# Three small pieces of softmax and value work moved off GpSimd in a hybrid mLSTM and sliding-window kernel

## The chip, the cores and the metric

The kernel runs on one core of one Trainium2 chip. The metric is the device time of one execution in microseconds (us); a lower one is better. Several executions are timed, and the median counts. One execution is also recorded by the hardware profiler, and its trace is what the views of the profile are drawn from. The engines are named as in the profile: PE (TensorE, matrix products), PEld (its loading of weights), DVE (VectorE), ACT (ScalarE), POOL (GpSimd) and SP (SyncE, which here issues most of the DMAs).

## The reference, cut to what matters

One layer of a streaming encoder is computed for a prompt of 2048 tokens and for a decoding batch of 8 sequences with 16 new tokens each. The input projection feeds two groups of heads: an mLSTM matrix memory (4 heads of 128), and a sliding-window attention (8 query heads, 2 key and value heads of 64, each query head with a learned sink). An output projection, a layer norm, a convolutional feed-forward part and a second layer norm follow. The two places that the change touches are these:

```python
# mLSTM, per chunk: the numerator and its normaliser
num = w_inter * (q @ C) + s @ v
den = w_inter * (q @ n) + sum(s, axis=-1)
h = num / max(abs(den), exp(-mt))

# attention with a sink
mx = max(max(s, axis=-1), sink)
p = exp(s - mx)
p = p / (sum(p, axis=-1) + exp(sink - mx))
o = p @ v
```

The kernel gets `den` from the same matrix product as `num`: it puts a column of ones behind the 128 columns of each head's values. It gets the sink's part of the sum by putting the sink into one more column behind the scores of the prompt's tiles, so that one exponential with a running sum covers both.

## The kernel before, in words

Tokens are handled in 17 tiles of 128: tiles 0 to 15 are the prompt, tile 16 (`NPT`) is the decoding batch. All products use float32 split into a high and a low part, three matmuls for one.

The work falls into stages. The input projection (L705 and L731 for its matmuls) goes through four blocks of tiles; the output projection (L223 to L225, called from `group`) through five; then come the up projection (L1874) and the down projection (L2081). These dense stages supply most of TensorE's work. The small work of the mLSTM and of the attention is cut into steps and woven into the dense stages by the class `Chains`. It keeps a clock of its own units, `t`: each piece of dense work (six matmuls in the input projection) adds 645 to it. Three chains wait to be stepped: `t_sample` (the decoding batch), `m_chain` (mLSTM, tile by tile) and `a_chain` (attention, tile by tile). A chain's step ends with `yield cost, delay` (and a number of PSUM banks that must be free): `cost` is added to the clock, and the chain is stepped again at the first piece of dense work at which the clock has passed the delay. `m_chain` and `a_chain` wait until `t_sample` is done.

So the order of TensorE's instructions is the order in which Python issues them, written out before the kernel runs (`manual_schedule` names PE alone). The other engines' instructions, and SP's DMAs, are put in order by the framework's scheduler, from the dependences and from the order of the program; every engine then works through its list in order. Tiles of one tag share a fixed number of buffers, and the framework puts in the waits that buffers and data need.

The output projection asks for finished tiles: `x_pair` (L893 issues its load) calls `chains.until(t)`, which steps the chains at once, without dense work between, if tile `t` isn't done. Block 3 of the output projection ends with a pair of tiles, and after the second of eight pieces of that pair's inner sum it asks for tiles 14 and 15.

The places of the change:

- `m_load` loads a tile's queries and keys, values and output gate. L1092 takes a tile `v1` of 4 heads by 129 columns from two buffers, L1093 issues the DMA of 128 columns of each head, L1094 lets GpSimd fill the four last columns with ones. `m_tile` reads `v1` at L1212 and L1221, and `t_sample` at L1438; `weighted` (L1424) takes two more tiles of the tag `v1`.
- `swa` handles one prompt tile of attention in two calls of `scores`, each for four of the eight heads. L1298 lets GpSimd copy the sink (four values per partition) behind the scores; L1304 is the score matmul, L1308 moves scores with mask and maximum to SBUF on VectorE, L1311 forms the negative maximum. `exps` (L1316) takes the exponentials with their sum on ScalarE, `divided` (L1319 the reciprocal, L1321 the scaled copies on ScalarE) divides, L1343 transposes on TensorE, L1344 copies the transposes and L1349 multiplies by the values.
- `swa_sample` does the attention of the decoding batch in two halves of four sequences. L1500 and L1501 are the score matmuls, L1502 to L1508 the maximum, L1509 the exponentials, L1510 and L1511 the sum and its reciprocal, L1512 the division by GpSimd for all four sequences in one instruction (128 partitions x 4 x 144), L1513 the step's end, L1518 and L1519 the transposes.

Of the kernel before, what the change touches and what calls it, by code (L numbers as in the profile page):

```python
# [10 lines left out]
AF = mybir.ActivationFunctionType  # L11
# [3 lines left out]
P = 128  # L15
# [5 lines left out]
NPT = SEQ // P  # L21
NT = NPT + 1
TOK = NT * P
MH = 4
# [181 lines left out]
class Prog:  # L206
# [881 lines left out]
    def m_load(self, t, b, ti):  # L1088
        nc = self.nc
        qk = self.work("qk", [P, 8, P], bufs=2)  # L1090
        nc.sync.dma_start(qk, self.zqk[b][:, :, ti * P:(ti + 1) * P].rearrange("f p m -> p f m"))
        v1 = self.work("v1", [P, MH, 129], bufs=2)  # L1092
        nc.sync.dma_start(v1[:, :, :P], self.zv[t].rearrange("p (h e) -> p h e", h=MH))  # L1093
        nc.gpsimd.memset(v1[:, :, P:129], 1.0)  # L1094
        og = self.work("og", [P, MH, P])
        nc.sync.dma_start(og, self.zog[t].rearrange("p (h e) -> p h e", h=MH))
        return qk, v1, og
# [174 lines left out]
    def swa(self, t):  # L1272
        nc = self.nc
        V = nc.vector
        if self.a_first is None:
            self.swa_first(t)
            yield 550, 4000, 2
        qh, ql = self.a_first
        self.a_first = None
        r = t % RING  # L1280
        if t == 0:
            slots, nk = [0], 1
            mask = self.mswa[:, :P]
            sel = slice(0, 1)
        else:
            slots, nk = sorted([(t - 1) % RING, r]), 2
            mask = self.mswa[:, P:] if slots[1] == r else self.mswa[:, :2 * P]
            sel = slice(slots[0], slots[1] + 1, slots[1] - slots[0])
        N = nk * P
        mix = self.work("mixa", [P, 4, P])  # L1290

        def scores(j0):

            sink, nsink = [x.rearrange("p (k j) -> p k j", k=2)[:, :, j0:j0 + 2] for x in (self.sink, self.nsink)]
            sc = self.work("sc", [P, 4, 2 * P + 4], bufs=2)
            mx, sm = [self.work(n, [P, 4], bufs=2) for n in ("amx", "asm")]
            w = lambda x: x.rearrange("p (k j) -> p k j", k=2)
            nc.gpsimd.tensor_copy(sc[:, :, N:N + 1].rearrange("p (k j) o -> p k (j o)", k=2), sink)  # L1298
            ps = [self.bank([P, 2, 2, P], "psc") for _ in range(2)]
            for j in range(2):  # L1300
                for i, (q, k) in enumerate(((qh, self.kh), (qh, self.kl), (ql, self.kh))):
                    for kvh in range(2):
                        rs = slice(64 * kvh, 64 * kvh + 64)
                        nc.tensor.matmul(ps[kvh][:, j, :nk], q[rs, j0 + j], k[rs, sel], start=i == 0, stop=i == 2)  # L1304
            for kvh in range(2):
                for j in range(2):
                    c = 2 * kvh + j
                    V.tensor_tensor_reduce(out=sc[:, c, :N], in0=ps[kvh][:, j, :nk].rearrange("p a b -> p (a b)"), in1=mask, scale=1.0, scalar=-3e38,  # L1308
                                           op0=ALU.add, op1=ALU.max, accum_out=mx[:, c:c + 1])

            V.scalar_tensor_tensor(w(mx), w(mx), -0.125, nsink, op0=ALU.mult, op1=ALU.min)  # L1311
            return sc, mx, sm

        def exps(sc, mx, sm):
            for j in range(4):
                nc.scalar.activation(sc[:, j, :N + 1], sc[:, j, :N + 1], AF.Exp, bias=mx[:, j:j + 1], scale=0.125, accum_out=sm[:, j:j + 1])  # L1316

        def divided(sc, mx, sm):
            V.reciprocal(sm, sm)  # L1319
            for j in range(4):  # L1320
                nc.scalar.activation(sc[:, j, :N], sc[:, j, :N], AF.Copy, scale=sm[:, j:j + 1])  # L1321

        z = [scores(0)]
        yield 900, 3200, 2
        exps(*z[0])
        z.append(scores(2))
        yield 900, 3600
        exps(*z[1])
        divided(*z[0])
        if t + 1 < NPT and self.i_done > self.place(t + 1)[0]:  # L1330
            self.a_load = self.swa_dma(t + 1)
        yield 0, 3000
        divided(*z[1])
        scs = [x[0] for x in z]
        yield 0, 4200, 2 + 2 * (self.a_load is not None)

        po = pts = None
        for kt in range(nk + 1):
            new = self.work("pth", [P, 2, 512], bufs=2) if kt < nk else None
            for kvh in range(2) if kt < nk else ():  # L1340
                pp = self.bank([P, 512], "ppt")
                for j in range(4):
                    nc.tensor.transpose(pp[:, j * P:(j + 1) * P], scs[j // 2][:, 2 * kvh + j % 2, kt * P:(kt + 1) * P], self.ident)  # L1343
                nc.scalar.copy(new[:, kvh], pp)  # L1344
            if kt:
                po = po or self.bank([P, 512], "ppo")
                for kvh in range(2):
                    w = self.kv[slots[kt - 1]][:, P + 64 * kvh:P + 64 * kvh + 64]
                    nc.tensor.matmul(po[64 * kvh:64 * kvh + 64], w, pts[:, kvh], start=kt == 1, stop=kt == nk)  # L1349
            pts = new  # L1350
            if kt == 0 and self.a_load is not None:

                self.swa_first(t + 1)
                self.chains.t += 550
            yield (860 if kt < nk else 0) + (1400 if kt else 0), 0 if kt == nk else 1500 if kt else 3000, 2 * (kt + 1 < nk) + (kt == 0)
        nc.scalar.copy(mix.rearrange("p a b -> p (a b)"), po)
        self.mix_out(t, 4, mix)
# [113 lines left out]
    def swa_sample(self, load, kvc):  # L1471
        nc, a = self.nc, self.a
        V = nc.vector
        t = NPT
# [9 lines left out]
        NK = P + DS  # L1484
        HB = DB // 2
        sk = self.sinkx.to_broadcast([P, HB])
        for half in range(2):
# [4 lines left out]
            sc = self.work("sc", [P, HB, NK], bufs=2, name="scs")  # L1492
            mx, es, sm = [self.work(n, [P, HB], bufs=2) for n in ("amx", "aes", "asm")]
            for b0 in (0, 2):
                ps = self.bank([P, 2, NK], "pscs")
                for i in range(2):
                    b = half * HB + b0 + i
# [11 lines left out]
                nc.scalar.activation(sc[:, b], sc[:, b], AF.Exp, bias=mx[:, b:b + 1], scale=0.125, accum_out=sm[:, b:b + 1])  # L1509
            V.tensor_add(sm, sm, es)  # L1510
            V.reciprocal(sm, sm)  # L1511
            nc.gpsimd.tensor_mul(sc, sc, sm.rearrange("p (b o) -> p b o", o=1).to_broadcast([P, HB, NK]))  # L1512
            yield 2700, 6500  # L1513
            pts = self.work("pth", [P, 2, HB, P], bufs=2, name="pts")
            pp = self.bank([P, HB, P], "ppt")
            pp2 = self.bank([DS, HB, P], "ppt2")
# [679 lines left out]
```

## Time and profile before

| | |
|---|---|
| median of 3 runs | 2306.43 us (2305.89 to 2309.27) |
| profiled execution, its own time | 2306.25 us |
| span of its trace | 2304.5 us |
| instructions | 39741 |
| granted TensorE clock, mean | 0.997 |

The span is what the trace covers, from its first to its last instruction; the execution's own time has some microseconds around it. A row of a view of groups gives line, engine, operation, the output and inputs by their names and shapes, the count, busy us and mean ns of one, and the idle time of the engine ahead of them with what ended it. A row of a timeline gives start and length in us; an idle time ahead of it and what ended it stand in brackets. In names, `scs` is the decoding batch's scores, `sc` the prompt tiles', `amx` the maxima, `asm` the sums, `v` the values with their ones, `ppt` the transposes' PSUM bank, `dps` the dense products' bank.

### The profile page before, as it was taken

What the parts mean: (1) busy time and instruction counts of PE and PEld (TensorE: products, weight loads), DVE (VectorE), ACT (ScalarE), POOL (GpSimd) and SP (SyncE); (2) the same over time, 40 slices, a digit from 0 to 9 for tenths busy, and PEclk for the clock granted to TensorE, in tenths of its full rate; (3) what the DMA queues carried; (4) which work ended last, traced back from release to release, by engine and by line L of the source; (5) the groups of instructions that cost most, each with busy time, mean ns of one, the idle gap of its engine ahead of it and who ended that gap; (6) DMA issues with size and microseconds to landing.
All of it is one profiled execution on the core that took longest, in us unless ns stands there. A gap on an engine that the chain in (4) does not pass through costs nothing.

```text
span 2304.5 us, 39741 instructions
## 1 busy us (share of the span) xinstructions
PE 2278.9 (99%) x14293; PEld 2094.4 (91%) x14293; DVE 1807.4 (78%) x3075; ACT 1272.4 (55%) x2377; POOL 279.4 (12%) x509
## 2 busy tenths in 40 slices
PE   8999999999999999999999999999999999999998
PEld 8999999989877778999999999999999978888876
DVE  8787587787688888998778777678766786895987
ACT  5453476776766656555656555556555544444442
POOL 0001001100011210211112101003111200200200
PEclk9999999999999999999999999999999999999999
DMA  7988999899987757888777888878998786746742
GB/s 267 319 306 297 309 322 342 310 306 341 309 286 239 242 199 277 302 328 300 277 281 272 307 304 310 306 256 289 316 299 260 248 299 213 253 170 223 253 156 83
DMA packets 300165, 632.38 MB, mean 274 GB/s; under 512 B 47868, under 2 KB 141120, under 8 KB 299968
## 3 DMA queue, kind: packets, MB, share of 16 engines
q1 hardware_dynamic: 295296, 616.14, 77.3%
q0 software_dynamic: 3520, 10.56, 1.4%
q10 hardware_dynamic: 1152, 3.15, 0.4%
q8 instruction: 113, 1.85, 0.3%
q14 instruction: 84, 0.69, 0.1%
HBM read 458.11 MB, written 171.64 MB: 273 GB/s over the span
## 4 chain that ended last, share of the span: by engine, by line
PE 81%; DVE 4%; DMA 2%; issue 1%; ACT 1%; POOL 0%; SPq 0%; DVEq 0%; ACTq 0%; POOLq 0%
PE dps L1874 19%; PE fup L1874 19%; PE dps L705 8%; PE fup L2081 6%; PE dps L2081 6%; PE fht L2081 6%; PE dps L223 3%; PE dps L224 2%; PE dps L225 2%; PE ppo L1349 1%; PE psc L1304 1%; PE ppt L1343 1%; PE dps L731 1%; PE fht L1698 1%; PE pscore L1129 1%
## 5 line engine op out<-in xcount | busy, mean ns | idle before, releaser
L1874 PE MATMUL fup<-hh,uw 128*128 128x384 f32 (+1 forms) x1848 | 478.4, 328 | 0.0
L1874 PE MATMUL dps<-hh,uw 128*128 128x384 f32 (+1 forms) x1848 | 478.0, 328 | 0.0
L1874 PEld LDWEIGHTS fup<-hh,uw 128*128 128x128 f32 x1848 | 330.5, 188 | 0.0
L1874 PEld LDWEIGHTS dps<-hh,uw 128*128 128x128 f32 x1848 | 330.3, 188 | 0.0
L1932 DVE SCALAR_TENSOR_TENSOR cc<-u,cw,cc 128x768 f32<-128x768 f32 (+1 forms) x264 | 258.2, 979 | 62.8 <-ACT cc L1930 56.1
L1874 PE MATMUL fup<-hl,uw 128*128 128x384 f32 (+1 forms) x924 | 303.2, 328 | 0.9 <-DVE hl L219 0.9
L1874 PE MATMUL dps<-hl,uw 128*128 128x384 f32 (+1 forms) x924 | 302.8, 328 | 0.0
L705 PE MATMUL dps<-w,oh 128*128 128x256 f32 x1344 | 254.2, 284 | 0.0
L218 ACT CAST uw<-wraw 128x1024 fp32r<-128x1024 f32 x126 | 123.3, 979 | 230.4 <-PE dps L2081 122.4
L219 DVE TENSOR_TENSOR w<-wraw,w 128x1024 fp32r<-128x1024 f32 (+2 forms) x167 | 189.7, 1142 | 66.0 <-ACT w L218 61.9
L218 ACT CAST w<-wraw 128x1024 fp32r<-128x1024 f32 (+2 forms) x167 | 163.0, 984 | 119.0 <-PE dps L705 61.9
L705 PEld LDWEIGHTS dps<-w,oh 128*128 128x128 f32 x1344 | 210.7, 188 | 10.8 <-issue 8.1
L219 DVE TENSOR_TENSOR uw<-wraw,uw 128x1024 fp32r<-128x1024 f32 x126 | 142.5, 1131 | 62.3 <-ACT uw L218 62.2
L705 PE MATMUL dps<-w,ol 128*128 128x256 f32 x672 | 188.1, 280 | 0.0
L1874 PEld LDWEIGHTS fup<-hl,uw 128*128 128x128 f32 x924 | 173.9, 188 | 1.7 <-DVE hl L219 1.5
L2081 PE MATMUL fup<-uw,fu 128*128 128x512 f32 x726 | 174.0, 396 | 1.2 <-ACT fht L2089 1.2
L1874 PEld LDWEIGHTS dps<-hl,uw 128*128 128x128 f32 x924 | 173.8, 188 | 0.0
L705 PE MATMUL dps<-oh,w 128*128 128x256 f32 x896 | 169.6, 285 | 3.6 <-DVE w L219 1.3
L2081 PEld LDWEIGHTS fup<-uw,fu 128*128 128x128 f32 x726 | 136.6, 188 | 34.3 <-ACT fht L2089 1.6
L2081 PE MATMUL dps<-uw,fu 128*128 128x512 f32 x660 | 165.3, 396 | 1.1 <-DVE uw L219 1.1
L1930 ACT ACTIVATE cc<-u,cw 128x768 f32<-128x768 f32 (+1 forms) x132 | 132.0, 1001 | 46.2 <-DVE u L1912 22.2
L2081 PEld LDWEIGHTS dps<-uw,fu 128*128 128x128 f32 x660 | 124.1, 188 | 31.2 <-DVE uw L219 1.5
(318 smaller groups left out, 4590.0 us busy)
## 6 DMA issues: line engine op xcount, KB each, us to landing
uw<-zw SPq DMA_DIRECT2D x176, 512.0 KB, 5.1
zw<-uw SPq DMA_DIRECT2D x88, 512.0 KB, 3.3
w<-zws SPq DMA_DIRECT2D x72, 512.0 KB, 5.8
wv<-wup SPq DMA_DIRECT2D x66, 512.0 KB, 4.4
wraw<-wi SPq DMA_DIRECT2D x65, 512.0 KB, 5.5
wraw<-zt SPq DMA_DIRECT2D x60, 512.0 KB, 4.1
wraw<-wdn SPq DMA_DIRECT2D x45, 512.0 KB, 4.5
wraw<-wo SPq DMA_DIRECT2D x40, 512.0 KB, 4.7
```

The costliest lines, as they stand in the source:

```text
L218: nc.scalar.copy(hi, src)
L219: return nc.vector.tensor_sub(lo, src, hi.bitcast(F32)).ins
L223: mm(out, ah, bh, start=start, stop=False)
L224: mm(out, ah, bl, start=False, stop=False)
L225: mm(out, al, bh, start=False, stop=stop)
L705: mm(o, l, r, start=s in (1, 7) and c == k == i == 0, stop=k == 3 and i == 2, skip_group_check=True)
L731: mm(o, x, w, start=k == i == 0, stop=k == KD - 1 and i == 2, skip_group_check=True)
L1129: self.nc.tensor.matmul(ps[:, h], qk[:, 4 + h], qk[:, h], start=True, stop=True)
L1874: mm(ps, l[:, k], r[:, k], start=s in (1, 7) and k == 0 and i == 0, stop=k == 3 and i == 2, skip_group_check=True)
L1930: S.activation(c[:, v], u[:, 2:2 + n], AF.Identity, bias=w[3], scale=w[2])
L1932: V.scalar_tensor_tensor(c[:, v], u[:, i:i + n], w[i], c[:, v], op0=ALU.mult, op1=ALU.add)
L2081: mm(ps, l[:, k, c], r[:, k], start=s in (1, 4, 7) and u == 0 and k == 0 and i == 0, stop=u == nu - 1 and k == n - 1 and i == 2, skip_grou ...
```

## The change

Three edits:

- The values' tiles are taken once and kept: one for the decoding batch (`t == NPT`, which comes first), and two at tile 0, which the prompt's tiles then use by turns. The columns of ones are filled when a tile is taken; each further load overwrites only the 128 value columns. There are 3 memsets in place of 17.
- The copy of the sink behind the scores goes from GpSimd, ahead of the score matmuls, to VectorE, behind the instruction that forms the negative maximum. There are 32 such copies, as before.
- The decoding batch's division goes from one GpSimd instruction for a half to four ScalarE copies scaled by a per-partition factor, one for each sequence, and the delay of the step that ends there goes from 6500 to 8500.

```diff
@@ m_load
-        v1 = self.work("v1", [P, MH, 129], bufs=2)
+        if t in (0, NPT):
+            self.v1 = [self.work("v1", [P, MH, 129], bufs=2) for _ in range(1 if t else 2)]
+            for v in self.v1:
+                nc.gpsimd.memset(v[:, :, P:129], 1.0)
+        v1 = self.v1[t % len(self.v1)]
         nc.sync.dma_start(v1[:, :, :P], self.zv[t].rearrange("p (h e) -> p h e", h=MH))
-        nc.gpsimd.memset(v1[:, :, P:129], 1.0)
@@ swa, scores
-            nc.gpsimd.tensor_copy(sc[:, :, N:N + 1].rearrange("p (k j) o -> p k (j o)", k=2), sink)
             ps = [self.bank([P, 2, 2, P], "psc") for _ in range(2)]
...
             V.scalar_tensor_tensor(w(mx), w(mx), -0.125, nsink, op0=ALU.mult, op1=ALU.min)
+            V.tensor_copy(sc[:, :, N:N + 1].rearrange("p (k j) o -> p k (j o)", k=2), sink)
             return sc, mx, sm
@@ swa_sample
             V.reciprocal(sm, sm)
-            nc.gpsimd.tensor_mul(sc, sc, sm.rearrange("p (b o) -> p b o", o=1).to_broadcast([P, HB, NK]))
-            yield 2700, 6500
+            for b in range(HB):
+                nc.scalar.activation(sc[:, b], sc[:, b], AF.Copy, scale=sm[:, b:b + 1])
+            yield 2700, 8500
```

## The prediction

> **What bounds the kernel now.** I read the page's totals first, then the chain that ended last, then what TensorE waited for.
>
> ```profile
> span 2304.5 us, 39741 instructions
> ...
> PE 2278.9 (99%) x14293; PEld 2094.4 (91%) x14293; DVE 1807.4 (78%) x3075; ACT 1272.4 (55%) x2377; POOL 279.4 (12%) x509
> ...
> PE 81%; DVE 4%; DMA 2%; issue 1%; ACT 1%; POOL 0%; SPq 0%; DVEq 0%; ACTq 0%; POOLq 0%
> ```
>
> TensorE (PE) is busy for 99% of the span and carries 81% of the chain; GpSimd (POOL), from which the change takes work, carries 0%. The change adds and removes no matmul. So it can win only idle time of TensorE, 2304.5 - 2278.9 = 25.6 us in all, and can lose only by making new idle time. The view of TensorE's waits says where that time is; after the names it gives total us, times, longest.
>
> ```profile
> engine line waited for: us in total, times, longest us
> PE ppt L1518 <- POOL v L1094: 2.9, 1, 2.9
> ...
> PE pnum L1212 <- issue: 1.9, 2, 1.4
> ...
> PE dps L705 <- ACT mr L1154: 0.8, 1, 0.8
> ...
> PE ppo L1349 <- ACT pth L1344: 0.6, 1, 0.6
> ```
>
> The longest single wait is at L1518, the transposes of the decoding batch's softmax. It is put down to the memset of L1094, but that is only what POOL finished last. The timeline of that place shows the true order (start, us, engine, line, operation).
>
> ```profile
> 243.06 0.39 PE L705 MATMUL dps<-w,oh 128*128 128x256 f32 x1
> ...
> 250.83 0.28 PE L705 MATMUL dps<-w,oh 128*128 128x256 f32 x1
> ...
> 252.44 0.18 DVE L1511 RECIPROCAL asm<-asm 128x4 f32<-128x4 f32 x1
> 252.76 1.15 POOL L1512 TENSOR_TENSOR scs<-scs,asm 128x576 f32<-128x576 f32 x1 [26.37 <-DVE asm L1511]
> 253.85 0.10 POOL L1094 MEMSET v<- 128x4 f32 x1
> ...
> 253.96 0.33 PE L1518 MATMUL ppt<-ident,scs 128*128 128x128 f32 x1 [2.85 <-POOL v L1094]
> ...
> 254.78 0.27 PE L1519 MATMUL ppt<-ident,scs 128*16 128x128 f32 x1
> ...
> 254.81 0.37 PE L705 MATMUL dps<-w,oh 128*128 128x256 f32 x1
> ...
> 254.98 0.59 ACT L1520 COPY pts<-ppt 128x512 f32<-128x512 f32 x1 [2.77 <-PE ppt L1518]
> ```
>
> TensorE ends its dense matmuls at 251.11 and stands still until 253.96, because the reciprocal ends at 252.62 and POOL's product, which the transposes read, ends at 253.91. That is the first half of the decoding batch. Nothing else that the diff touches shows as a wait of TensorE.
>
> **The change part by part.** *The batch's division and its due time.* How far does 8500 in place of 6500 move the transposes? The weave advances 645 of its units per six matmuls. The first step at or past 6500 is the 11th (7095), past 8500 the 14th (9030): three more dense steps, 18 matmuls. Their price is in the chain of work:
>
> ```profile
> 259.98 7.92 PE dps L705 x66
> ```
>
> That is 0.12 us each, so 11 steps are 7.92 us (the 243.06 to 251.11 above is 8.05, which fits) and three steps are 2.16 us. TensorE would reach the transposes at 251.11 + 2.16 = 253.27. When is ScalarE's (ACT's) product there? These shapes are near it, from the groups by form, and one run of four from the timeline:
>
> ```profile
> L1509 ACT ACTIVATE scs<-scs,amx 128x144 f32<-128x144 f32 x8 | 3.2, 404 | 1.0 <-DVE amx L1507 1.0
> L1167 ACT ACTIVATE hn<-hn,ms 128x128 f32<-128x128 f32 x68 | 22.0, 391 | 33.7 <-POOL ms L1161 33.7
> L566 ACT ACT_TABLE_LOAD x1 | 1.3, 1283 | 0.7 <-PEq L2188 0.7
> ...
> 785.96 1.28 ACT L1167 ACTIVATE hn<-hn,ms 128x128 f32<-128x128 f32 x4 [1.85 <-POOL ms L1161]
> ```
>
> One scaled copy of 128x144 is about 0.40 us and the next begins about 0.31 later ((1.28 - 0.39) / 3 = 0.30 for 128 columns, a little more for 144). Starting at 252.76 as POOL did, the four end at 253.16, 253.47, 253.78 and 254.09. POOL's one product ended at 253.91, so ScalarE is no faster in all, but the transposes go batch by batch and need only their own piece: TensorE's pairs take (254.81 - 253.96) / 4 = 0.21 us, start at 253.27, wait about 0.1 us each for the last two pieces, and end near 254.3. There 14 steps are done; before, they were done at 254.81 + 2.16 = 256.97. **Gain: 2.6 us** (at most the whole 2.85). It falls by 1.03 us for each cast that ScalarE puts between the exponentials and the copies, an order that this trace cannot show.
>
> The row with ACT_TABLE_LOAD bears on this part: one load in the whole execution, 1.28 us, although the prompt's tiles go from Exp (L1316) to Copy (L1321) and back with every pair of heads. If the step from Exp to Copy did load a table here, ScalarE's copies would begin 1.28 us later and half of the gain would go: 2306.25 - 1.3 = 2305.0. The Trainium skill, "ScalarE: Activation LUTs", section "What ACT_TABLE_LOAD costs", asks about 2.66 us for each switch to another set of functions, and by that, an estimate, the whole gain would go. The trace speaks against any switch here, since the same two functions already alternate without one; I count this with the first rival, at 0.01.
>
> The second half has room already:
>
> ```profile
> 269.10 0.26 PE L1501 MATMUL pscs<-ks,qs 64*64 64x16 f32 x4
> ...
> 272.98 1.03 ACT L218 CAST w<-wraw 128x1024 fp32r<-128x1024 f32 x1
> ...
> 273.14 1.40 POOL L1512 TENSOR_TENSOR scs<-scs,asm 128x576 f32<-128x576 f32 x1 [19.18 <-ACT zev L761]
> ...
> 274.04 1.57 DVE L219 TENSOR_TENSOR w<-wraw,w 128x1024 fp32r<-128x1024 f32 x1 [0.51 <-ACT w L218]
> ...
> 277.17 0.27 PE L1518 MATMUL ppt<-ident,scs 128*128 128x128 f32 x1
> ```
>
> POOL's product ends at 274.54 and the transposes come at 277.17. Behind the cast, ScalarE would end at 274.01 + 1.33 = 275.3, still early, and the transposes come three steps later besides. Cost 0. What is late next: both halves together put the tiles' chains six steps (4.3 us) further back in the dense stream. That costs nothing as long as they end before the output projection's block needs tile 15. They have that room:
>
> ```profile
> 857.85 1.08 PE L1349 MATMUL ppo<-pth,kva 128*64 128x512 f32 x4
> ...
> 864.71 0.69 DVE L1613 SCALAR_TENSOR_TENSOR ymix<-ymix,dps 128x512 f32<-128x512 f32 x1 [0.40 <-PE dps L225]
> ```
>
> The chain's last matmuls end at 858.9. The last pair of tiles starts near 864.4 and asks for tile 15 only after four of its sixteen sets of three matmuls, so 5.5 us are left at the least, against a move of 4.3. The last input's loads move with it, and lie under that pair.
>
> *The sink column and the ones.* The rows are these: POOL's copy and memset, VectorE's (DVE's) nearest small instruction, and the long instruction in front of which or behind which it can land.
>
> ```profile
> L1298 POOL COPY sc<-k_sink 128x4 f32<-128x4 f32 x32 | 12.5, 395 | 43.4 <-PE ppt L1343 35.9 <-PE ppt L1519 3.8 <-DMA wraw<-zws 3.3
> L1094 POOL MEMSET v<- 128x4 f32 x17 | 1.8, 104 | 111.5 <-PE pcu L1221 106.9 <-PE pnum L1438 4.3 <-POOLq L2188 0.3
> ...
> L1311 DVE SCALAR_TENSOR_TENSOR amx<-amx,nsink 128x4 f32<-128x4 f32 x32 | 4.7, 146 | 0.1
> ...
> L219 DVE TENSOR_TENSOR w<-wraw,w 128x1024 fp32r<-128x1024 f32 (+2 forms) x167 | 189.7, 1142 | 66.0 <-ACT w L218 61.9
> ```
>
> POOL loses 12.5 us of copies, 14 of 17 memsets (1.5 us) and 2.5 us of products; it is 12% busy, so this frees nothing that is late. VectorE gains 32 copies. A VectorE copy of this shape is not in the trace: I take the 0.15 us of L1311, the same four columns, with below it 0 (it slips into a gap) and above it 0.15 + 1.14 = 1.3 us (one long subtraction gets in front of it). In sum 4.7 us on an engine with 22% free; TensorE pays only where the exponentials, which now wait for that copy, have no slack before their transposes at L1343. The products' DMA into the lasting tiles waits for the readers of two tiles ago, as the old tiles' did, so SP's queue stands as before. Cost 0.
>
> **Sum.** 2306.25 us (this execution, span 2304.5 and 1.75 around it) - 2.6 = 2303.65. The median shown is 0.18 above that execution, so **2303.8 us**.
>
> **The rivals.** *The wait stays:* ScalarE runs two or more casts before the copies, or the moved chains meet new small waits of the same size. Against it: ScalarE had been idle for 2.77 us when it began at 254.98, so nothing was waiting to be put there. For it: in the second half a cast did slip in. It gives 2306.4.
>
> *Slower, by the sink's copy:* place, the chain copy, exponentials, division, transposes of a prompt tile. Here are the last division on ScalarE and the first transposes on TensorE of tiles 1, 10 and 14.
>
> ```profile
> 355.52 1.71 ACT L1321 ACTIVATE sc<-sc,asm 128x256 f32<-128x256 f32 x4 [0.98 <-DVE asm L1319]
> 362.45 1.04 PE L1343 MATMUL ppt<-ident,sc 128*128 128x128 f32 x8
> ...
> 681.32 1.71 ACT L1321 ACTIVATE sc<-sc,asm 128x256 f32<-128x256 f32 x4 [1.20 <-DVE asm L1319]
> 681.57 1.85 PE L1343 MATMUL ppt<-ident,sc 128*128 128x128 f32 x8
> ...
> 814.22 1.71 ACT L1321 ACTIVATE sc<-sc,asm 128x256 f32<-128x256 f32 x4
> 815.71 1.04 PE L1343 MATMUL ppt<-ident,sc 128*128 128x128 f32 x8
> ```
>
> Tile 1 has 5.2 us of slack; tiles 10 and 14 have none, and tile 10's transposes already take 1.85 us in place of 1.04. With 1.3 us for each of two halves such a tile loses 2.6 us; two tiles lose 5.2. It decides where slack is under 2.6 us. 2306.4 - 2.6 + 5.2 = 2309.0, and each further tight tile adds 2.6.
>
> *Faster by more:* the shifted chains and the emptier POOL queue also end the other waits of the tiles' stage in the list above, 1.9 + 0.8 + 0.6 = 3.3 us. 2303.8 - 3.3 = 2300.5. For it: the subtraction at 274.04 beside POOL's product took 1.57 us against a mean of 1.14. The Trainium skill, "GPSIMD Engine Reference", "Key points", says that POOL shares its SBUF interfaces with VectorE and contends with instructions of two SBUF inputs; that row agrees. Against it: none of those waits names POOL, and only 16.5 us of POOL's work go.
>
> **How the numbers follow.** Forecast 0.60, the wait stays 0.13, slower 0.14, faster by more 0.13. About 0.2% (4.6 us) is what a measurement of this kernel can tell from no change: the lines are 2301.8 and 2311.0. Faster: all of the last rival and 0.05 of the forecast, which its own scatter of about 1.5 us carries over, 0.18. Slower: 0.08 of the slower rival, with three or more tight tiles. Within: 0.74. The range goes from the faster rival less half a us, 2300.0, to the slower one with two tight tiles, 2309.5.
>
> **What would show it.** Right: no wait over 0.5 us at L1518, its transposes three steps (18 matmuls) later, four ACT instructions of about 0.4 us each where POOL's product was; tile chains end about 4 us later against the dense work; POOL's instructions 509 - 32 - 2 - 14 = 461. Wrong: a cast between L1509 and the division, waits of TensorE at L1343 that point to ScalarE's division, or waits of TensorE behind 858 that name the last tile's output. A result past 2311 would mean that reordering of the engines' queues, not these instructions, sets the time.

## The result and the profile after

The changed kernel takes 2332.19 us in the median of 6 runs (2325.68 to 2334.22), the kernel before 2306.62 us in 6 runs beside it (2305.79 to 2309.27). The ratio is 1.0105, 95% interval 1.0093 to 1.0116: 1% slower, past the upper end of the range. The profiled execution took 2329.14 us.

The page of the changed kernel begins so (busy time, share of the span, instructions of each engine):

```profile
span 2327.3 us, 39622 instructions
...
PE 2289.6 (98%) x14293; PEld 2098.8 (90%) x14293; DVE 1812.0 (78%) x3107; ACT 1271.2 (55%) x2385; POOL 251.4 (11%) x461
```

The span grew by 22.8 us. TensorE stands idle for 2327.3 - 2289.6 = 37.7 us in place of 25.6, so 12.1 us of the loss are new waits; the other 10.7 us are matmuls that took longer (2289.6 - 2278.9). GpSimd has the 461 instructions that were forecast. The view of TensorE's waits (total us, times, longest) shows which waits are new:

```profile
PE dps L705 <- ACT dps L800: 4.0, 1, 4.0
PE ppt L1346 <- ACT sc L1324: 3.9, 3, 2.7
PE fht L1702 <- DMA hst<-zh: 3.1, 1, 3.1
PE fht L1702 <- ACT hraw L1703: 2.6, 1, 2.6
...
PE ppt L1522 <- ACT scs L1516: 1.1, 1, 1.1
```

The wait at the decoding batch's transposes (now L1522) fell from 2.85 to 1.1 us. The first four rows are not in the list of before; that list has one wait of over 2 us, the 2.85. To see when the time goes, I took the start of the same instruction in both traces and subtracted:

```
instruction                                     before    after   behind by
ACT COPY dps, just ahead of the batch           241.03   240.68    -0.4
the same, just behind the batch's first half    267.87   266.00    -1.9
the same, some 100 us later                     364.77   368.40    +3.6
the same                                        471.21   476.85    +5.6
the same                                        500.98   510.28    +9.3
first transposes of the last stage (fht)        877.66   892.33   +14.7
second cast of their result (hh)                890.53   913.00   +22.5
end of the span                                2304.5   2327.3    +22.8
```

The batch gained 1.5 us. Then 5.5 us go near 338, 3.7 us near 485 and 7.8 us between 878 and 913; some 7.4 us more go in smaller pieces between these places.

**Near 338.** One timeline of all engines (start, length in us; in brackets the idle time ahead and what ended it):

```profile
334.16 3.09 POOL L1164 TENSOR_TENSOR ms<-mr,mhalf 128x4 f32<-128x4 f32 x1 [16.42 <-DVE mr L1163]
...
337.29 0.40 ACT L1170 ACTIVATE hn<-hn,ms 128x128 f32<-128x128 f32 x1 [4.21 <-POOL ms L1164]
337.60 0.58 ACT L800 COPY dps<-dps 128x512 f32<-128x512 f32 x1
...
338.23 0.58 PE L705 MATMUL dps<-oh,w 128*128 128x256 f32 x1 [4.02 <-ACT dps L800]
```

TensorE's dense matmuls need a PSUM bank that ScalarE empties at L800. That copy stands in ScalarE's list behind the scaling of an mLSTM tile (L1170), and the scaling waits 4.21 us for a power that GpSimd works out (L1164). So ScalarE has an instruction ready to run and can't get to it, and TensorE stands for 4.02 us. In the kernel before the same scaling of the same tile waits for GpSimd too, 2.89 us, but what TensorE needs then isn't stuck behind it for long:

```profile
333.76 0.69 ACT L1167 ACTIVATE hn<-hn,ms 128x128 f32<-128x128 f32 x2 [2.89 <-POOL ms L1161]
...
335.13 0.58 ACT L800 COPY dps<-dps 128x512 f32<-128x512 f32 x1
```

Part of the 4.02 us is GpSimd itself: the power took 3.09 us here, against 1.36 us at this tile in the kernel before. Why it was slower was not taken apart. The windows around the wait (busy us and instructions of each engine, then granted clock, DMA share, GB/s) show a second price:

```profile
335.00:340.00 5.00, 1.77 (x7) 1.55 (x8) 2.63 (x5) 2.71 (x8) 2.26 (x1) 0.78 0.98 349
340.00:345.00 5.00, 5.00 (x22) 3.06 (x23) 2.12 (x3) 3.76 (x11) 0.00 (x0) 0.54 0.45 152
345.00:350.00 5.00, 5.00 (x46) 4.69 (x43) 2.97 (x12) 3.27 (x10) 0.00 (x0) 1.00 0.95 316
```

Behind the wait TensorE runs at a clock of 0.54 for the next 5 us: it is 5.00 us busy with 22 matmuls, where the slice after it does 46.

**Near 485** it is the same pattern with another victim: the scaling at L1170 waits 1.58 us for GpSimd's power, the last two divisions of a prompt tile (L1324) stand behind it, and TensorE's transposes at L1346 wait 2.71 us for them.

```profile
482.93 0.89 ACT L1324 ACTIVATE sc<-sc,asm 128x256 f32<-128x256 f32 x2
485.40 1.28 ACT L1170 ACTIVATE hn<-hn,ms 128x128 f32<-128x128 f32 x4 [1.58 <-POOL ms L1164]
486.59 0.89 ACT L1324 ACTIVATE sc<-sc,asm 128x256 f32<-128x256 f32 x2
```

The clock goes to 0.80 and 0.86 in the slices 485 to 490 and 490 to 495. A wait of 1.03 us just ahead, at 483.49, is for the two divisions before the scaling and isn't of this pattern.

**Between 878 and 913** the last stage begins. Its eight loads of the hidden state (`hst`) start only when the last tile's attention output has been stored (`zmix<-mixa`): the stage takes its memory when that of the chains is closed, and in all 17 traces the first load is issued 2.4 to 3.2 us after that store. First the queues of before, SP's and ScalarE's:

```profile
859.62 0.38 SPq L1171 DMA_DIRECT2D zmix<-mixa  x1
```

```profile
862.44 0.34 ACTq L1716 DMA_DIRECT2D hst<-zh  x1
...
875.29 0.33 ACTq L1716 DMA_DIRECT2D hst<-zh  x1
```

And of the changed kernel:

```profile
881.22 0.37 SPq L1174 DMA_DIRECT2D zmix<-mixa  x1
```

```profile
883.60 0.37 ACTq L1720 DMA_DIRECT2D hst<-zh  x1
...
896.09 0.55 ACTq L1720 DMA_DIRECT2D hst<-zh  x1
896.68 1.07 ACT L1703 COPY hraw<-fht 128x512 f32<-128x512 f32 x2 [5.19 <-DMA hst<-zh]
```

Between the store and the first transposes lie 877.66 - 859.62 = 18.0 us in the kernel before and 892.33 - 881.22 = 11.1 us here. In the kernel before the DMA engines were as full:

```profile
870.00:875.00 5.00, 5.00 (x23) 4.07 (x22) 1.91 (x3) 3.14 (x4) 0.00 (x0) 1.00 1.04 410
```

But there the 18.0 us covered it. Here the loads are late, and fall together with other transfers:

```profile
885.00:890.00 5.00, 5.00 (x23) 4.08 (x22) 1.92 (x2) 2.68 (x4) 0.00 (x0) 1.00 0.99 350
890.00:895.00 5.00, 4.76 (x25) 3.59 (x23) 4.27 (x6) 1.18 (x2) 0.00 (x0) 1.00 1.03 409
895.00:900.00 5.00, 2.69 (x10) 1.91 (x11) 0.00 (x0) 2.79 (x4) 0.00 (x0) 0.76 0.98 358
900.00:905.00 5.00, 2.69 (x13) 1.87 (x11) 2.44 (x2) 1.51 (x3) 0.00 (x0) 0.90 0.94 383
```

From 885 to 905 the DMA engines are busy all the time (share 0.94 to 1.03, up to 409 GB/s); TensorE waits 2.56 and 3.07 us and the clock falls to 0.76 in one slice.

**Why do these places differ?** None of them is at a line that the change edits. But the delay of 8500 moves the start of the batch's second half by three steps, and with it every later step that the weave puts between dense matmuls. Counting the dense matmuls ahead of an instruction in the order that each kernel writes out for TensorE:

```
                                             before   after
scores of the batch's second half              1671    1689
state update (pcu) of tiles 0, 1, 2            2031    2049
                                               2229    2253
                                               2415    2439
last tile: last transposes of the mLSTM        4395    4371
last tile: last attention products (ppo)       4401    4431
```

The chains do not simply move back. The batch's own last transposes (L1518) come 36 matmuls later (1737 to 1773), the six steps of the forecast; the first tiles come 18 to 24 later; by the last tile the mLSTM is 24 earlier and the attention 30 later (the slice 885 to 890 above has 23 matmuls in 5 us, so 30 are 6.5 us, near the 18.0 - 11.1 = 6.9 us above).

### The profile page after: what moved, and what is told of

The parts are those of the page before. It is cut to its first block, busy times and chain, and to the rows that moved or that the text cites. A ratio compares the mean times of both kernels' runs of the same rounds, so it can differ in the third digit from the quotient of the medians.

```text
span 2327.3 us, 39622 instructions
## 1 busy us (share of the span) xinstructions
PE 2289.6 (98%) x14293; PEld 2098.8 (90%) x14293; DVE 1812.0 (78%) x3107; ACT 1271.2 (55%) x2385; POOL 251.4 (11%) x461
## 5 line engine op out<-in xcount | busy, mean ns | idle before, releaser
L705 PEld LDWEIGHTS dps<-oh,w 128*128 128x128 f32 x896 | 143.0, 192 | 12.5 <-ACT dps L800 4.2
```

The costliest lines, as they stand in the source:

```text
L705: mm(o, l, r, start=s in (1, 7) and c == k == i == 0, stop=k == 3 and i == 2, skip_group_check=True)
```

## The experiments

**Theory:** the later due time makes the loss. It re-weaves the tiles' chains into the dense work, and in the new order ScalarE's list puts needed work behind a scaling that waits for GpSimd (338, 485), and the last tile's attention ends too late for the last stage's loads. **Rival:** the moved work makes it: the sink's copies on VectorE, or the divisions on ScalarE.

### The due time alone, and all but the due time

The kernel before with 8500, and the changed kernel with 6500:

```diff
@@ e1: before        and the reverse in e2: the changed kernel
-            yield 2700, 6500
+            yield 2700, 8500
```

> The kernel before with one number changed: the delay after the decoding batch's division is 8500 in place of 6500; the division, the sink's copy and the ones stay on GpSimd. Theory A (the later due time re-weaves the tiles' chains against the dense matmuls, and the new order makes TensorE wait): 2328 to 2334 us, with waits of TensorE over 2.5 us near 338, 487 and 897 us of the span, as in the changed kernel. Rival B (the work moved to VectorE and ScalarE fills their lists and delays what TensorE reads): 2303 to 2307 us, without those waits.

> The changed kernel with the delay put back to 6500: all three pieces of work moved off GpSimd, TensorE's order that of the kernel before. Theory A: 2304 to 2308 us, the wait at the batch's transposes still 2 to 2.9 us, no wait over 2 us between 300 and 900 us. Rival B: 2325 to 2334 us, with the waits of the changed kernel.

Measured: the due time alone gives 2333.37 us (ratio 1.0115, interval 1.0098 to 1.0132), all but the due time 2308.26 us (1.0003, 0.9991 to 1.0014); before took 2306.52 beside them. The waits of TensorE in the first have the same places as in the changed kernel:

```profile
PE ppt L1343 <- ACT sc L1321: 4.9, 3, 2.7
PE dps L705 <- ACT dps L800: 4.3, 1, 4.3
PE fht L1698 <- DMA hst<-zh: 3.3, 2, 2.3
PE fht L1698 <- ACT hraw L1699: 2.1, 1, 2.1
```

So the whole loss is the due time's, and the rival falls. All but the due time is neither faster nor slower.

### Other due times

```diff
@@ the changed kernel, two runs
-            yield 2700, 8500
+            yield 2700, 7800    (9200 in the other)
```

> The changed kernel with the delay at 7800: the batch's transposes come two dense steps later than before, but every tile's matmuls stand at the same dense matmul as in the kernel before. If the place of the tiles' chains is what cost the time: 2303 to 2307 us, the wait at the batch's transposes 1.1 to 2 us. If any later delay costs: over 2315 us.

> The changed kernel with the delay at 9200, later still than 8500. Here the two chains keep the step of the kernel before (186 dense matmuls a tile in the input projection's last block, where 8500 gives 180), some 30 to 42 matmuls later there, and the last attention matmuls come 9 dense matmuls later than before, where 8500 gives 30. If the loss grows with the delay: over 2334 us. If it hangs on how the chains fall against the dense work: 2304 to 2318 us, the loss at the output projection's end gone.

7800 leaves the prompt's tiles at their old places in TensorE's list but for two small transposes, and takes 2307.11 us (1.0008, 0.9999 to 1.0016). 9200 is later than 8500 and takes 2317.01 us (1.0049, 1.0036 to 1.0061): less than half the loss. The waits for the last stage's loads did not go, as the second theory had it: 4.0 us of them are left. So the loss doesn't grow with the delay. It depends on which order comes out.

### The scaling off ScalarE's list

```diff
@@ m_scaled, the changed kernel
-            self.nc.scalar.activation(hn[:, h], hn[:, h], AF.Copy, scale=s[:, h:h + 1])
+            self.nc.vector.tensor_scalar_mul(hn[:, h], hn[:, h], s[:, h:h + 1])
```

> The changed kernel, with the mLSTM output's scaling (four copies a tile, which read GpSimd's power) moved from ScalarE to VectorE; TensorE's order is untouched. Theory: at about 338 and 487 us of the span ScalarE stands, in its order, at that scaling and waits for GpSimd, and the copy or the division that TensorE needs is behind it. Then the waits put down to L800 (4.0 us) and to the attention's division (3.9 us) fall under 1.5 us each and the slow clock behind them goes: 8 to 15 us faster than the changed kernel, 2317 to 2324 us. Rival (VectorE or GpSimd is simply late there, whoever scales): the waits stay within 1 us of what they were, 2329 to 2335 us.

2322.34 us, 9.85 less than the changed kernel by the medians and 7.4 by the ratios (against before 1.0073, 1.0060 to 1.0085). The wait at L800 is gone, and so is the dip of the clock:

```profile
335.00:340.00 5.00, 3.14 (x24) 2.06 (x22) 4.75 (x12) 3.52 (x10) 0.18 (x1) 1.00 0.96 350
340.00:345.00 5.00, 5.00 (x44) 4.66 (x43) 4.04 (x14) 2.75 (x8) 0.00 (x0) 1.00 0.96 296
```

The instruction that waits for GpSimd now waits in VectorE's list, and ScalarE's copy at L800 goes ahead: it starts at 333.13, before GpSimd's power does (333.83). That settles the places at 338 and 485: an instruction that waited for another engine, with needed work behind it. What is left of the loss is at the last stage, and some new waits for VectorE (1.9 and 1.6 us for `ql`, the first of them at 339, close to the wait that went).

### The last stage's loads

First, the stage's transposes six pieces of dense work later, and then the loads from GpSimd's queue in place of ScalarE's, both in the changed kernel:

```diff
@@ e7: the stage's first pieces (f_hT, f_tokens) are stepped six pieces later
-                if i >= 2:
+                if i >= 8:
...
-                if i in (4, 7, 10):
+                if i in (10, 13, 16):
...
@@ e11: all eight loads (two lines, this is one)
-                        nc.scalar.dma_start(w[at[0][0]][:, at[0][1]:at[0][1] + 2], z)
+                        nc.gpsimd.dma_start(w[at[0][0]][:, at[0][1]:at[0][1] + 2], z)
```

> The changed kernel, with the transposes that feed the up projection, and the splits behind them, begun six pieces of dense work later in the output projection's last block. If the last loss (near 897 to 906 us of the span) is a wait for loads that come late because the tile chains end later, it goes: both waits there gone, 5 to 9 us faster than the changed kernel, 2323 to 2328 us. If the loss there is something else (the output projection itself held up), the time stays at 2329 to 2334 us.

> The changed kernel, with the eight loads for the first transposes of the up projection issued from GpSimd's queue in place of ScalarE's, where they stand between casts. Theory C (they are late because ScalarE's list holds them behind casts that wait for the last tile's output): the waits of TensorE at these transposes (2.6 and 3.1 us) go, 5 to 9 us faster than the changed kernel, 2323 to 2327 us. Theory D (they are late because the memory they fill is held by the tiles' chains until the last one ends): the waits stay, 2329 to 2335 us.

Later transposes: 2329.45 us (1.0096, 1.0082 to 1.0109), 2.7 less than the changed kernel, not 5 to 9; the waits there fell from 5.6 to 3.7 us. Loads from GpSimd's queue: 2331.58 us (1.0110, 1.0097 to 1.0123), no gain. There the loads were all issued by 888.5, but each took longer to land (median us from issue to landing in the last column; first the changed kernel, then this one):

```profile
hst<-zh ACTq DMA_DIRECT2D x4, 512.0 KB, 8.3
```

```profile
hst<-zh POOLq DMA_DIRECT2D x4, 512.0 KB, 10.5
```

So the queue isn't the cause. The DMA engines are as full as in the changed kernel (share 0.96 to 1.02 from 885 to 905), so an earlier issue is largely paid back in longer transfers: the waits at the transposes fell only from 5.6 to 4.3 us, and waits of 1.6 us at L225 (0.7 in the changed kernel) and 1.2 us at L224 stand elsewhere, at 696 and 834.

Next, the chain's end itself: the last tile's attention products due at once, in one step (18 of the 30 matmuls earlier, e13) or in two (all 30, e16), each also with the scaling on VectorE (e14, e17):

```diff
@@ swa, the changed kernel: e13, e14; e16 and e17 do it at the step before too (3000)
-        yield 0, 4200, 2 + 2 * (self.a_load is not None)
+        yield 0, 4200 if t + 1 < NPT else 0, 2 + 2 * (self.a_load is not None)
```

> The changed kernel, but the last tile's attention products (alone of all tiles') are due at once, so that they stand about 18 matmuls earlier in TensorE's list. Theory (the end of the last tile's chain sets when the last stage's eight loads start, and these then land too late): the loads start about 4 us earlier, the waits of TensorE at L1702 fall from 5.6 us to under 2, and it is 4 to 8 us faster than the changed kernel: 2324 to 2328. The two waits behind GpSimd's power at 334 and 483 stay. Rival (the loads are late for a reason of their own): 2329 to 2335.

> The changed kernel with the scaling of the mLSTM's tiles on VectorE and the last tile's attention products due at once. If the losses are two separate ones, they add: no wait at L800 and L1324 behind the scaling, waits at L1702 under 2 us, 2314 to 2319. If the end of the last tile is not what delays the loads, as with the scaling alone: 2320 to 2324.

e13 took 2331.08 us (1.0100, 1.0084 to 1.0116), e14 2320.90 us (1.0065, 1.0050 to 1.0080): 1.1 and 1.4 us less than without the edit, so this missed. The loads of e13 did start 5.7 us earlier (877.88; 2.2 of the 5.7 this run was ahead already at 850), but the eighth was issued at 895.43, against 896.09:

```profile
877.88 0.37 ACTq L1720 DMA_DIRECT2D hst<-zh  x1
...
895.43 0.33 ACTq L1720 DMA_DIRECT2D hst<-zh  x1
```

That left open whether the place of those products is the cause at all. The sharpest test is to do it to the kernel before, alone: the same products, with their transposes, 30 matmuls later. Nothing else in TensorE's list moves but the last tile's mLSTM transposes, by 9 matmuls.

```diff
@@ swa, e15: the kernel before
-        yield 0, 4200, 2 + 2 * (self.a_load is not None)
+        yield 0, 4200 if t + 1 < NPT else 10500, 2 + 2 * (self.a_load is not None)
```

> The kernel before, with the last tile's attention products 30 matmuls later in TensorE's list, where the changed kernel has them, and nothing else moved. Theory (that place alone makes the handover's loss): the eight loads start some 14 us later, waits of 4 to 7 us at L1698, and it is 5 to 9 us slower than before: 2311 to 2316. Rival (the handover's loss comes from the other moved work): 2306 to 2309.

> The changed kernel with the last tile's attention products due at once in two steps, so that they stand where the kernel before has them. Theory: the loads start over 10 us earlier, the waits at L1702 go, and it is 6 to 9 us faster than the changed kernel: 2323 to 2326; less by as much as ScalarE's divisions of the last tile are now late. Rival (the products' place is not the cause): 2329 to 2334.

> The same with the scaling of the mLSTM's tiles on VectorE as well. If these two are the whole loss: 2308 to 2315, no wait at L800, L1324 behind the scaling, or L1702 over 1 us. If a third of it lies elsewhere: 2316 to 2321.

e15 took 2313.68 us against 2305.45: 8.2 us slower (1.0038, 1.0025 to 1.0051). TensorE's waits in it are those of the changed kernel's last stage, beside the batch's own wait, which it shares with the kernel before (second row):

```profile
PE fht L1698 <- ACT hraw L1699: 3.8, 1, 3.8
PE ppt L1518 <- POOL v L1094: 2.8, 1, 2.8
PE fht L1698 <- DMA hst<-zh: 2.6, 1, 2.6
```

So the place of the last tile's last steps alone makes this loss. The runs form a series. From the start of the last attention products to the first transposes of the last stage, and the waits at the transposes:

```
                                              us between   waits there, us
before                                             19.8         0
changed, both steps at once (e16, e17)             19.8         0, 0
due time 9200                                      17.7         4.0
changed, one step at once (e13, e14)               17.0         3.3, 5.2
changed, transposes later (e7)                     16.3         3.7
changed; before with late products (e15)           12.9         5.6, 6.3
due time alone (e1); scaling on VectorE (e9)       12.9         5.5, 7.1
changed, loads from GpSimd (e11)                   12.9         4.3
```

With 19.8 us the loads are in time, with 17.7 and less they aren't: e7 and e13 brought little because they gave back too little. But e16 took 2327.05 us (1.0088, 1.0071 to 1.0105), 5.1 less than the changed kernel and not 6 to 9, and its interval overlaps the changed kernel's. Part of what is missing is that the hurried transposes of the last tile now wait for their own divisions: the waits at L1346 went from 3.9 to 5.6 us.

```profile
PE ppt L1346 <- ACT sc L1324: 5.6, 4, 2.7
```

e17, with both repairs, took 2316.45 us (1.0046, 1.0031 to 1.0061), 15.7 us less than the changed kernel and 5.9 less than with the scaling alone (e9). That is past the 2315 expected if these two were the whole loss, and within what was expected if a third of it lies elsewhere. 11.0 us over before remain, among them a new wait of 2.4 us at L1346 near 856 and waits for VectorE, to which the scaling was given. In its trace TensorE stands idle only 2.3 us longer than before (27.9 us in place of 25.6), and its matmuls take 6.0 us longer. What share of the 11 us the repairs themselves cost wasn't taken apart. The two named causes are shown; that they are the whole loss is not.

### The batch's wait without the re-weave

If 8500 is given to the first half alone, and the second half's last step comes forward by as much, the prompt's tiles keep their places. With the whole change (e8), and with nothing else of it, GpSimd dividing as before (e10):

```diff
@@ swa_sample: e8 in the changed kernel, e10 in the kernel before
-            yield 2700, 6500
+            yield 2700, 6500 if half else 8500
...
-            yield 1000, 500 if half else 7000
+            yield 1000, 500 if half else 5000
```

> The changed kernel, but only the first half's delay is 8500; the second half keeps 6500, and the pause after the first half is 5000 in place of 7000, so that the second half and all the tiles' chains come at the same dense matmul as in the kernel before. Theory A: the wait at the transposes falls under 1.2 us and nothing else moves, 2303 to 2305.5 us, 1 to 2.7 us faster than the kernel before. Rival B: near the changed kernel, over 2320 us.

> The kernel before, with its division on GpSimd, but the first half's transposes due at 8500 and the second half's last step brought forward by as much, so that the tiles behind stay where they were. Theory (the later due time itself covers GpSimd's product, and all else stays): the wait at L1518 goes from 2.85 to under 0.8 us, 2303.5 to 2305.5. Rival (the batch's wait only hands its time to the next ones): 2306 to 2308.

e8 took 2306.65 us (1.0003, 0.9994 to 1.0012): the loss is gone, but of the gain of 1 to 2.7 us nothing came, a miss. e10 took 2304.33 us against 2306.98 (ratio 0.9990, 0.9982 to 0.9999): the one version that beats the kernel before, by about 2.7 us, as expected; the interval, 0.2 to 4.2 us, just excludes no gain. TensorE's waits, e8 first, then e10:

```profile
PE ppo L1352 <- ACT pth L1347: 1.9, 1, 1.9
PE pht L1180 <- DVE ql L219: 1.6, 1, 1.6
...
PE ppt L1522 <- ACT scs L1516: 1.1, 1, 1.1
```

```profile
PE ppo L1349 <- ACT pth L1344: 0.9, 1, 0.9
...
PE pht L1177 <- DVE ql L219: 0.8, 1, 0.8
...
PE ppt L1518 <- POOL scs L1512: 0.7, 1, 0.7
```

At the batch's transposes, e10 waits 0.7 us for GpSimd and e8 1.1 us for ScalarE. ScalarE's order in the changed kernel shows why:

```profile
252.09 1.05 ACT L218 CAST w<-wraw 128x1024 fp32r<-128x1024 f32 x1 [0.23 <-PE dps L705]
...
253.04 0.59 ACT L761 ACTIVATE zev<-dps 128x512 f32<-128x512 f32 x1
...
253.53 1.32 ACT L1516 ACTIVATE scs<-scs,asm 128x144 f32<-128x144 f32 x4
...
253.99 0.33 PE L1522 MATMUL ppt<-ident,scs 128*128 128x128 f32 x1 [1.11 <-ACT scs L1516]
```

A cast and an activation of 0.59 us stand between the exponentials (the last begins at 251.37) and the four scaled copies, which take 1.32 us. GpSimd had nothing in front. And e8 has 1.9 and 1.6 us of waits in tiles where e10 has 0.9 and 0.8. To see whether these come with the sink's copies, the kernel before with that edit alone:

```diff
@@ scores, the kernel before
-            nc.gpsimd.tensor_copy(sc[:, :, N:N + 1].rearrange("p (k j) o -> p k (j o)", k=2), sink)
...
+            nc.vector.tensor_copy(sc[:, :, N:N + 1].rearrange("p (k j) o -> p k (j o)", k=2), sink)
```

> The kernel before with the sink column copied by VectorE alone, its division and due time untouched. By the prediction's forecast for this part it is free: 2305.5 to 2307. By its slower rival, waits of 1 to 2.6 us appear at the attention products of some tiles: 2307.5 to 2309.5.

2309.78 us against 2306.98; ratio 1.0008, 0.9999 to 1.0017, so between no change and 4 us slower: not settled. Its wait at L1349 is 1.9 us, as in e8, where before had 0.6. So that wait does come with the sink's edit; the 1.6 us for `ql` does not show in this run, and its cause stays open. A cost of the sink's edit in time is likely, but too small for these runs.

## Why the prediction was wrong

- **What bounds the kernel** held: TensorE's idle time and its matmuls are the time, and the loss is read from its waits. What I left out is that a wait can also make the matmuls behind it longer: "can lose only by making new idle time" misses 10.7 of the 22.8 us.
- **Three steps, 18 matmuls later** was exact (1671 to 1689). **Four scaled copies of about 1.33 us** was exact too (1.32). **The gain of 2.6 us** came to 1.5: the cast that the text said an order of ScalarE might put there did stand there, with an activation of 0.59 us besides. ScalarE's idle time of 2.77 us in the old order was no argument against it: the cast waits for dense matmuls, and the three steps put ahead of the transposes let it start at 252.09 in place of 256.39. No second table load appeared. With GpSimd dividing, e10 shows about the forecast gain, so the later due time was the useful part of the edit and ScalarE's copies were not needed for it.
- **The step that failed** is "both halves together put the tiles' chains six steps (4.3 us) further back in the dense stream. That costs nothing as long as they end before the output projection's block needs tile 15". It took a weave of discrete steps for a shift by one amount. The runs show in its place: the batch's end moved the six steps, the first tiles only 18 to 24 matmuls; the mLSTM and the attention of the last tile moved in opposite directions, by 24 and 30 matmuls; the attention's 6.5 us are over the 5.5 us that I called room; and what came due first was not tile 15 but the last stage's loads (e15: 8.2 us for that alone). Ahead of that, the new order put needed work of ScalarE behind a scaling that waits for GpSimd (e9: 7 to 10 us for these places). I counted the move at its end only and not at each of the meetings on the way.
- **The sink and the ones at 0:** the copy took 0.16 us (forecast 0.15), and its cost is at most 4 us, not settled above 0. With the old due time, all the moved work together is within 0.2% (e2), so as a part of this result the step stands. GpSimd's busy time fell by 28.0 us (279.4 to 251.4), not by the 16.5 of the sum; 11.0 of it are its 51 powers, which ran shorter in the mean though the one at 334 ran longer.
- **The rivals:** the slower one named the sink's copies as mechanism, and the waits at the prompt tiles' transposes that it foresaw did come, but the due time alone has them too. "The wait stays" came half true, by ScalarE's cast. "Faster by more" did not come.
- **What would make it wrong** had the right sentence ("reordering of the engines' queues, not these instructions, sets the time"), and it got no chance of its own. With a step moved in a static order ahead of 16 tiles, it should have been a rival with a price.

## What to carry to other kernels

Where the order of an engine is written out ahead of time by due times, changing one due time is a change to every later step: list the places of the later steps in both orders, and look at what each one meets, before pricing the instruction itself. An instruction that waits for another engine holds up all that stands behind it on its own engine, so ask of each such wait what the bounding engine needs from that list next. And keep a local repair local: the same delay, paid back within its own chain (e10), kept the gain and left the rest where it was.

## What the runs showed of the hardware

The clock behind a wait was the surprise. The wait of 2.85 us at the batch's transposes is the same in the kernel before and in e15. First before, then e15 (granted clock is the third number from the end):

```profile
252.00:254.00 2.00, 0.04 (x1) 0.04 (x1) 0.34 (x2) 0.21 (x2) 1.19 (x2) 1.00 0.82 272
254.00:256.00 2.00, 2.00 (x18) 1.93 (x19) 0.00 (x0) 1.02 (x2) 0.00 (x0) 1.00 1.00 388
```

```profile
250.00:252.00 2.00, 0.67 (x3) 0.55 (x4) 0.00 (x0) 0.00 (x0) 1.19 (x2) 0.68 0.94 348
252.00:254.00 2.00, 2.00 (x12) 1.82 (x10) 0.00 (x0) 0.88 (x2) 0.00 (x0) 0.50 0.72 268
```

In before the clock stays at 1.00 and TensorE does 18 matmuls in the first 2 us behind the wait; in e15 it runs at 0.50 and does 12. So a wait of this length sometimes costs itself alone and sometimes some 1.3 us more (half of the 0.67 and the 2.00 us that TensorE is busy in these two slices).

The clock records of the traces show when. In each of the 17 traces the granted clock changes only at instants that lie whole multiples of 3.41 us apart; they cut the trace into steps, and a fall to half lasts one or two steps. The fall goes with how long TensorE stood idle within one step. In before such an instant, at 252.53, cuts the wait of 2.85 us into 1.42 and 1.44 us, and the clock stays. In e15 2.22 us of the wait lie in the step that ends at 250.70, and the clock falls there. In the changed kernel the 3.07 us at 905 are cut into 1.72 and 1.34 us and the clock stays, while 2.63 us in one step at 487 and a whole step of 3.41 us at 337 bring it down to half. Over all traces, from 60 to 2260 us and of the steps at full clock:

```
idle time of TensorE within a step     steps   followed by half clock
1.87 us or more                           29                       29
1.37 to 1.87 us                           28                        6
under 1.37 us                          10856                        0
```

The ends of matmuls are modelled in these traces, so the bounds are rough. But the length of a wait alone does not tell its price: how it falls on these steps matters too, and that differs from trace to trace. In that stretch the kernel before has no step at half clock, and the changed kernel has four (13.65 us: two behind 338, one each at 488 and 898). An estimate from that: half of it, up to 6.8 us, of the 10.7 us by which its matmuls took longer. e17 has two such steps, up to 3.4 of its 6.0 us.

The Trainium skill, "TensorE: Matmul & The Clock Gate", section "What's actually happening", says that the clock halves after an idle window of about 3.4 us, and that the window runs freely. The steps of 3.41 us, on which the same wait can fall either way, agree with a window that runs freely; that 1.87 us of idle time within one step were enough does not agree with a whole idle window of 3.4 us, and here the measurement decides.
